# Half of a modulation in the output projection, transposes two tiles late, and six heads' softmax sums divided out of the gates

## The chip, the cores and the metric

The kernel runs on 1 core of one Trainium2 chip. The metric is the device time of one execution in microseconds (us); lower is better. A core has five engines with a queue of instructions each: TensorE (PE in the profile; its weight loads are PEld), VectorE (DVE), ScalarE (ACT), GpSimd (POOL), and SyncE (SP), which here issues the DMAs.

## The reference, cut to what matters

Two layers of a diffusion backbone, width 1024. There are 512 latent tokens and 256 context tokens (the context is updated in layer 0 only). Of each layer:

```
hx = rmsnorm(x) * (1 + scale_x) + shift_x        # shift, scale, gate = silu(c) @ w_ada + b_ada
px = hx @ w_in                                   # a_k a_v b_k b_v a_q b_q a_z b_z g_a g_b
qa, ka = rmsnorm per head; qb, kb = rope(rmsnorm per head)
a_att = neighbourhood attention of 8 heads, plus all context keys   # softmax(q k / 8 + bias) v
b_att = grouped attention of 8 query heads on 2 key heads           # softmax(q k / 8) v
o_a = (a_att * silu(a_z)) @ w_o_a;  o_b = (b_att * silu(b_z)) @ w_o_b
out = (sigmoid(g_a) * o_a + sigmoid(g_b) * o_b) @ w_out
x = x + gate_x * out
```

The context takes the same path in layer 0 with its own vector c_ctx and context keys alone. The shift and scale of layer 1 are needed when layer 1's hx is made, which is at the end of layer 0; its gate only at the end of layer 1.

## The kernel before, in words

**Products.** Every product with a weight is done in three passes (L346 to L348): both operands are split into a rounded high part and a low part. A weight tile of 128x512 arrives by DMA as `raw` (three buffers), ACT writes `whi` (L316, L331), and DVE or POOL writes `wlo` (L319, L333; `mix_lo` gives odd tiles to DVE, even ones to POOL). `tok_proj` (L356) makes 128 tokens by 512 columns in 24 matmuls; `chan_proj` (L362) makes channels by tokens. Results lie in PSUM tiles `psf` and `psx`, six in all outside the attentions.

**Stages of a layer.** (1) Products for a_k, a_v and a_q. A tile of a_k or a_q goes through `head_rstd` (ACT squares L386, DVE sums L388, POOL L253 and L255), a multiplication on DVE (L392), four transposes on PE and a copy on ACT (`to_channels`, L396 to L417). (2) Neighbourhood attention, below. (3) Products for b_k, b_v and b_q; these tiles get their rotation on DVE and POOL (`rope_heads`, L443 to L456) before the transposes. (4) Grouped attention. (5) The merge: products with w_o_b, then the output projection with w_out: two halves n of 512 columns with nt = 6 tiles of tokens each in layer 0; a finished tile is multiplied by the gate and added to x on DVE (L984, L986), and in the second half each tile's next-layer hx is made (`make_hx`, L258 to L279: ACT sum of squares, POOL, DVE y at L265, eight transposes L271 on PE, ACT with shift and scale, DVE split).

**An attention.** `pipeline` (L794) goes through 8 heads: scores of head h, then the values of head h-1, then some of `fill`, the independent products (gates a_z, b_z, g_a, g_b and, later, w_o_a), which are there to keep PE at work. For each of four query tiles, and two context tiles in layer 0, DVE takes the maximum (L755, L901, L687), ACT the exponentials with their sum `r` (L758, L903, L691), and `softmax_tail` (L607) scales p by 0.5/r: reciprocal on DVE (L609), then either one DVE operation (L612) or, for query tiles 1 and 3, two POOL operations (L614, L615). Then p is transposed on PE (L623, L625), split by ACT and DVE (`pth` L628, `ptl` L629), and multiplied with v (L778 to L789, L918, L919, L702, L703). `head_out` (L632) adds two halves and multiplies the gate z by the result on POOL (L639). The tiles p come from a pool of 7 buffers (neighbourhood attention, layer 0), 8 (layer 1) or 10 (grouped attention).

**The modulation.** Layer 1's shift and scale are 16 tiles of 128 outputs, and the 1024 inputs are taken in two halves. Of each half `ada_steps` (L200) makes 32 `dot` steps: a 256 KB tile `rawb` of w_ada is loaded (two buffers), and DVE multiplies and sums it with the row of c and the row of c_ctx, one step each (L222; the step with c_ctx overwrites rawb). The first half runs beside the products a_v and a_q of layer 0, the second half beside its neighbourhood attention (L831), followed by `ada_mod` (L237). The gate's 8 tiles run beside the grouped attentions.

**What sets the order.** A scheduler orders each engine's instructions when the program is built, by its own estimates of their durations; engines then run their queues strictly in that order. So an instruction whose input is late holds up everything behind it on its engine, SP's queue of DMAs included. Dots are pinned behind the last DVE instruction written before them.

Of the kernel before, what the change touches and what calls it, by code (L numbers as in the profile page):

```python
# [28 lines left out]
NA_POOL = (1, 3)  # L29
GQ_POOL = (1, 3)  # L30
# [17 lines left out]
def hybrid_kernel(es: ExitStack, tc, x, ctx, cvec, w_ada, w_ada0, small, gvec, w_in, w_o_a, w_o_b, w_out,  # L48
# [48 lines left out]

    x0, ctx0 = x[0], ctx[0]
# [4 lines left out]
    cd = drp.tile([16, 128], F32, name="cd")  # L103
    gs = [drp.tile([128, 4, NTOK], F32, name=f"gs{c}") for c in range(4)]
# [95 lines left out]
    def ada_steps(l, tiles, halves, nv, pool):  # L200
# [13 lines left out]
        def dot(h, i, v):  # L214
            if v == 0:
                load_tile(h, i)
            w = cb["w"]
            o = w if v == nv - 1 else pool.tile([128, 512], BF16, tag="junk", name=nm("junk"), bufs=1)
            ins = nc.cur_bb.bb.instructions
            before = next(j for j in reversed(ins) if j.engine == mybir.EngineType.DVE)  # L220
            n = len(ins)
            V.tensor_tensor_reduce(o, w, cb[h][:, v, :], 1.0, 0.0, ALU.mult, ALU.add, asum[:, i, h, v:v + 1])  # L222
            for j in nc.cur_bb.bb.instructions[n:]:
                if j.engine == mybir.EngineType.DVE:
                    tc.add_manual_dep(j, before.name, mybir.DependencyInfo(
                        mybir.DependencyClass.NoSync, mybir.DependencyReason.DATA), reason="program order")
# [151 lines left out]
    hp = {}  # L378
# [17 lines left out]
    def to_channels(y, npair, dst, t, perm, g):  # L396
# [46 lines left out]
    def rope_heads(npair, ps, rs, ta, tb, dst, t):  # L443
# [4 lines left out]
        r = hp["p"].tile([128, 512], F32, tag="rr", name=nm("rr"), bufs=2)  # L448
# [11 lines left out]
    def layer(l, hx, nxt, mid):  # L460
# [100 lines left out]
        if first:  # L561
# [13 lines left out]
            for t in range(6):  # L575
                ev(t, pss[t])
            bg = ada_steps(1, range(16), (0,), 2, hp["p"])
# [22 lines left out]
        for t in range(qt):  # L600
            tok_proj(w, 512, a_hx, t, evac_na(qav, True, gq, 5 if first else 2))
            run(bg, per_bg)
        run(bg, len(bg))
        bgp_es.close()

        if True:
            def softmax_tail(p, n, r, pieces, eng=None):  # L607

                V.reciprocal(r, r)  # L609
                for i, (c0, c1) in enumerate(pieces):  # L610
                    if eng is None:
                        V.tensor_scalar(p[:, c0:c1], p[:, c0:c1], r[:, i:i + 1], 0.5, ALU.mult, ALU.mult)  # L612
                    else:
                        G.tensor_scalar(r[:, i:i + 1], r[:, i:i + 1], 0.5, None, ALU.mult)  # L614
                        G.tensor_tensor(p[:, c0:c1], p[:, c0:c1],  # L615
                                        r[:, i:i + 1].to_broadcast([128, c1 - c0]), ALU.mult)
# [63 lines left out]
            def ctx_scores(q, kh, kl):  # L680
# [8 lines left out]
                r = sp.tile([128, 2], F32, tag="r", name=nm("r"), bufs=8)  # L689
                for i in range(2):  # L690
                    S.activation(p[:, 256 * i:256 * i + 256], pss[:, 256 * i:256 * i + 256], AF.Exp,  # L691
                                 bias=mx[:, i:i + 1], accum_out=r[:, i:i + 1])
                softmax_tail(p, 512, r, [(0, 256), (256, 512)])
# [25 lines left out]
            run(fill, PRE_NA * len(spans))  # L719
# [15 lines left out]
            def na_scores(h, q, kh, kl):  # L735
                load_bias(h)
                ps_ = []
                for i in range(4):
# [4 lines left out]
                    else:  # L743
# [7 lines left out]
                        for kk, b in ((kh, True), (kl, False)):  # L751
# [5 lines left out]
                    r = sp.tile([128, 2], F32, tag="r", name=nm("r"), bufs=8)  # L757
                    S.activation(p[:, :512], p[:, :512], AF.Exp, bias=mx[:, 0:1], scale=-1.0,  # L758
                                 accum_out=r[:, 0:1])
                    softmax_tail(p, 512, r[:, 0:1], [(0, 512)], G if i in NA_POOL else None)  # L760
# [33 lines left out]
            def pipeline(fill, spread, scores_of, values_of, last=None, bg=[]):  # L794
# [305 lines left out]
```

## Time and profile before

| | |
|---|---|
| Time, 3 runs | 1178.5 us median (1177.02 to 1178.72) |
| The profiled execution's own time | 1175.41 us |
| Span of the profiled execution | 1173.6 us |
| Granted TensorE clock, mean | 0.998 |
| PE matmuls | 6078 |
| DVE busy / POOL busy | 810.4 us / 507.5 us |
| ACT busy | 574.6 us |

The span runs from the first to the last instruction. Busy is the time in which an engine has an instruction in work. The matmuls' ends are modelled and matmuls overlap, so a PE that is shown busy may still have been held up for a little. "Idle before" is the time that an engine stood still ahead of an instruction, with what ended it. L-numbers are lines of the kernel before.

### The profile page before, as it was taken

What the parts mean: (1) busy time and instruction counts of PE and PEld (TensorE: products, weight loads), DVE (VectorE), ACT (ScalarE), POOL (GpSimd) and SP (SyncE); (2) the same over time, 40 slices, a digit from 0 to 9 for tenths busy, and PEclk for the clock granted to TensorE, in tenths of its full rate; (3) what the DMA queues carried; (4) which work ended last, traced back from release to release, by engine and by line L of the source; (5) the groups of instructions that cost most, each with busy time, mean ns of one, the idle gap of its engine ahead of it and who ended that gap; (6) DMA issues with size and microseconds to landing.
All of it is one profiled execution on the core that took longest, in us unless ns stands there. A gap on an engine that the chain in (4) does not pass through costs nothing.

```text
span 1173.6 us, 17342 instructions
## 1 busy us (share of the span) xinstructions
PE 1128.1 (96%) x6078; PEld 948.4 (81%) x6078; DVE 810.4 (69%) x1512; ACT 574.6 (49%) x1175; POOL 507.5 (43%) x463
## 2 busy tenths in 40 slices
PE   5999989899999999999999999999999999999898
PEld 4688878788997888878788887887888878877686
DVE  4557699986474599888583465339777657798573
ACT  4453254566452455576430264436656445756531
POOL 3362355453277244364410136336554764655311
PEclk9999999999999999999999999999999999999999
DMA  9534323321251443370240322413322525452133
GB/s 372 194 111 135 105 81 106 113 75 61 82 157 62 131 135 110 71 282 19 71 165 25 135 72 80 127 34 98 105 77 68 170 71 190 143 181 90 37 129 96
DMA packets 88128, 134.05 MB, mean 114 GB/s; under 512 B 10756, under 2 KB 52712, under 8 KB 86376
## 3 DMA queue, kind: packets, MB, share of 16 engines
q1 hardware_dynamic: 88040, 132.94, 35.4%
q8 instruction: 48, 0.79, 0.3%
q14 instruction: 40, 0.33, 0.1%
HBM read 115.58 MB, written 17.32 MB: 113 GB/s over the span
## 4 chain that ended last, share of the span: by engine, by line
PE 71%; DVE 14%; POOL 5%; issue 4%; ACT 3%; DMA 1%; DVEq 0%; POOLq 0%; ACTq 0%
PE psx L346 10%; PE psx L347 10%; PE psx L348 10%; PE psf L346 8%; PE psf L347 8%; PE psf L348 8%; PE pst L625 4%; DVE ptl L629 2%; PE pss L674 2%; PE pss L675 2%; PE psv L919 1%; POOL rsb L255 1%; DVE rawb L222 1%; DVE mx L901 1%; DVE qs L668 1%
## 5 line engine op out<-in xcount | busy, mean ns | idle before, releaser
L333 POOL TENSOR_TENSOR wlo<-raw,whi 128x512 fp32r<-128x512 f32 x64 | 91.5, 1432 | 121.9 <-ACT whi L331 101.8
L629 DVE TENSOR_TENSOR ptl<-pst,pth 128x512 fp32r<-128x512 f32 (+1 forms) x176 | 115.8, 671 | 40.8 <-ACT pth L628 39.8
L346 PE MATMUL psf<-hx,whi 128*128 128x512 f32 (+1 forms) x368 | 138.9, 378 | 1.1 <-DVE za L483 1.0
L347 PE MATMUL psf<-hx,whi 128*128 128x512 f32 (+1 forms) x368 | 138.3, 376 | 0.0
L348 PE MATMUL psf<-hx,wlo 128*128 128x512 f32 (+1 forms) x368 | 137.9, 375 | 0.0
L628 ACT CAST pth<-pst 128x512 fp32r<-128x512 f32 (+1 forms) x176 | 98.7, 577 | 79.4 <-PE pst L625 55.7
L346 PE MATMUL psx<-whi,hx 128*128 128x512 f32 (+1 forms) x368 | 136.4, 372 | 0.0
L347 PE MATMUL psx<-wlo,hx 128*128 128x512 f32 (+1 forms) x368 | 136.1, 370 | 0.0
L348 PE MATMUL psx<-whi,hx 128*128 128x512 f32 (+1 forms) x368 | 133.7, 370 | 0.0
L319 POOL TENSOR_TENSOR wlo<-raw,whi 128x512 fp32r<-128x512 f32 (+1 forms) x52 | 66.6, 1281 | 153.7 <-ACT whi L316 131.5
L316 ACT CAST whi<-raw 128x512 fp32r<-128x512 f32 (+1 forms) x112 | 64.7, 592 | 103.5 <-PE psx L348 36.5
L331 ACT CAST whi<-raw 128x512 fp32r<-128x512 f32 x128 | 78.0, 620 | 54.4 <-DMA raw<-in_w_in_dram 38.0
L625 PE MATMUL pst<-ident,p 128*128 128x128 f32 x640 | 100.3, 273 | 3.4 <-DVE ptl L629 1.1
L625 PEld LDWEIGHTS pst<-ident,p 128*128 128x128 f32 x640 | 77.8, 140 | 16.5 <-DVE p L612 1.3
L333 DVE TENSOR_TENSOR wlo<-raw,whi 128x512 fp32r<-128x512 f32 x64 | 63.9, 999 | 35.6 <-ACT whi L331 35.1
L615 POOL TENSOR_TENSOR p<-p,r 128x512 f32<-128x512 f32 (+1 forms) x64 | 86.3, 1348 | 5.2
L614 POOL TENSOR_SCALAR r<-r 128x1 f32<-128x1 f32 x64 | 24.5, 383 | 135.2 <-DVE r L609 127.3
L346 PEld LDWEIGHTS psf<-hx,whi 128*128 128x128 f32 x368 | 69.5, 189 | 12.9 <-DVE za L483 1.7
L319 DVE TENSOR_TENSOR wlo<-raw,whi 128x512 fp32r<-128x512 f32 (+1 forms) x60 | 49.5, 828 | 43.1 <-ACT whi L316 42.3
L346 PEld LDWEIGHTS psx<-whi,hx 128*128 128x128 f32 x368 | 69.4, 189 | 11.8 <-issue 0.8
L348 PEld LDWEIGHTS psf<-hx,wlo 128*128 128x128 f32 x368 | 69.4, 189 | 11.6
L348 PEld LDWEIGHTS psx<-whi,hx 128*128 128x128 f32 x368 | 69.6, 189 | 11.2
(239 smaller groups left out, 3068.1 us busy)
## 6 DMA issues: line engine op xcount, KB each, us to landing
raw<-in_w_in_dram SPq DMA_DIRECT2D x160, 256.0 KB, 2.9
rawb<-in_w_ada_dram SPq DMA_DIRECT2D x64, 256.0 KB, 2.7
gs<-zt SPq DMA_DIRECT2D x32, 256.0 KB, 2.4
raw<-in_w_out_dram SPq DMA_DIRECT2D x32, 256.0 KB, 2.6
tg<-gs SPq DMA_DIRECT2D x4, 1536.0 KB, 7.1
rawx<-in_w_ada_dram SPq DMA_DIRECT2D x4, 1024.0 KB, 6.5
rawy<-in_w_ada_dram SPq DMA_DIRECT2D x4, 1024.0 KB, 12.2
raw<-in_w_o_a_dram SPq DMA_DIRECT2D x16, 256.0 KB, 3.1
```

The source lines that it names most:

```text
L316: S.copy(hi[:, :n], raw[:, :n])
L319: e.tensor_tensor(lo[:, :n], raw[:, :n], F(hi[:, :n]), ALU.subtract)
L331: S.copy(hi, raw)
L333: lo_eng(i).tensor_tensor(lo, raw, F(hi), ALU.subtract)
L346: T.matmul(ps, lhs[0], rhs[0], start=first, stop=False)
L347: T.matmul(ps, lhs[0], rhs[1], start=False, stop=False)
L348: T.matmul(ps, lhs[1], rhs[0], start=False, stop=last)
L614: G.tensor_scalar(r[:, i:i + 1], r[:, i:i + 1], 0.5, None, ALU.mult)
L615: G.tensor_tensor(p[:, c0:c1], p[:, c0:c1], r[:, i:i + 1].to_broadcast([128, c1 - c0]), ALU.mult)
L625: T.transpose(pt[:, c0:c0 + 128], src, ident)
L628: S.copy(hi[:, n0:n1], pt[:, n0:n1])
L629: V.tensor_tensor(lo[:, n0:n1], pt[:, n0:n1], F(hi[:, n0:n1]), ALU.subtract)
```

## The change

Three things are changed, and a few buffer counts with them.

1. The second half of layer 1's modulation (one load of the rows c, 32 dots, `ada_mod`) leaves layer 0's neighbourhood attention and goes into layer 0's output projection: 6 steps after each of the first tiles of half n = 0, so that all are written there. Dots are now pinned by the new helper `behind`, which does for any engine what the old lines did for DVE.
2. The transposes of a_k, a_q, b_k and b_q are written later: `to_channels` puts them in a list, and `tok_proj` writes out the oldest when more than two wait, so that a tile's transposes stand two products behind its own product (in layer 0 from a_q on; a_k's six there stay where they were). They are pinned on PE behind the last PE instruction written before them. At the end of a stage the remaining two follow the first fill pieces.
3. For heads 0 to 5 of each attention the exponentials stay unscaled. The sums of a pair of heads are collected in one tile r; `invert` makes 0.5/r on DVE, `sums_out` turns it by one PE transpose, copies it on ACT and writes it to DRAM by a DMA on ACT's queue; a head later `normalise` reads it back with SP DMAs that repeat each head's row on 64 partitions, into a buffer of the pool of p, and POOL multiplies the pair's gated output z by it. Heads 6 and 7 scale every tile of p on DVE; POOL scales none.

```diff
+    def behind(fn):
...
+    def turn_late(n):
+        while len(hp["late"]) > n:
+            after_products(hp["late"].pop(0))
-    def to_channels(y, npair, dst, t, perm, g):
+    def to_channels(*a):
+        hp["late"].append(lambda: turn(*a))
+    def turn(y, npair, dst, t, perm, g):
...
         tok_mm(ps, w, n, a, t, 0, KT)
         evac(t, ps)
+        turn_late(hp["lag"])
...
-                tok_proj(w, 512, a_hx, t, evac_na(kav, False, gk))
+                tok_proj(w, 512, a_hx, t, evac_na(kav, False, gk, 4))
...
+        for i in range(PRE_NA * len(spans)):
+            run(fill, 1)
+            turn_late(1 if i == 0 else 0)
+        turn_late(0)
...
-            def softmax_tail(p, n, r, pieces, eng=None):
-                V.reciprocal(r, r)
...
+            def scale(h, p, r, c0, c1):
+                if h > 5:
+                    V.reciprocal(r, r)
+                    V.tensor_scalar(p[:, c0:c1], p[:, c0:c1], r, 0.5, ALU.mult, ALU.mult)
+            def invert(r):
+                n = 6 if first else 4
+                V.tensor_scalar(r[:, 0:n], r[:, 0:n], 2.0, None, ALU.mult)
+                V.reciprocal(r[:, 0:n], r[:, 0:n])
+            def sums_out(j, r):
+                n = 12 if first else 8
+                pt = psw(128, "t")
+                T.transpose(pt[0:n], r[:, 0:n // 2].rearrange("p j e -> p (j e)"), ident)
+                row = p_tile()[:, 0:128]
+                S.copy(row[0:n], pt[0:n])
+                S.dma_start(rd[j][0:n], row[0:n])
+            def normalise(j, z, perm):
...
+                    rb = p_tile()[:, 0:128 * (j1 - j0)]
+                    for e in range(2):
+                        nc.sync.dma_start(rb[64 * e:64 * e + 64].rearrange("p (j q) -> p j q", q=128),
+                                          rd[j].rearrange("(j e) q -> e j q", e=2)[e:e + 1, j0:j1]
+                                          .to_broadcast([64, j1 - j0, 128]))
...
+                        G.tensor_tensor(zp, zp, rb, ALU.mult)
...
                     if prev is not None:
                         values_of(h - 1, prev)
+                    if h % 2 and h < 7:
+                        invert(att["r"])
+                        sums_out(h // 2, att["r"])
+                    elif h % 2 == 0 and h:
+                        behind(lambda: normalise(h // 2 - 1, z, perm))
...
-            bg = ada_steps(1, range(16), (1,), 2, att["p"]) + [lambda: ada_mod(1)] if first else []
-            run(bg, 1)
-            pipeline(fill, 9, na_first, values_of(za, na_values), bg=bg)
+            pipeline(fill, 9, na_first, values_of(za, na_values), za, True)
...
-            run(fill, PRE_GQ * len(spans))
+            for i in range(PRE_GQ * len(spans)):
+                run(fill, 1)
+                turn_late(1 if i == 0 else 0)
...
+            bg = ada_steps(1, range(16), (1,), 2, mp) + [lambda: ada_mod(1)] if first else []
+            run(bg, 1)
+            per_bg = -(-len(bg) // nt)
             for n in range(2):
...
                     tok_proj(w, 512, a_m, t, evac_o)
+                    run(bg, per_bg)
                     run(late, len(late) - 1)
```

More of the change, by code (lines that the diff above doesn't have):

```diff
@@ L103, in hybrid_kernel @@
     cd = drp.tile([16, 128], F32, name="cd")
+    rd = [drp.tile([12, 128], F32, name=f"rd{i}") for i in range(4)]
     gs = [drp.tile([128, 4, NTOK], F32, name=f"gs{c}") for c in range(4)]
@@ L218, in dot @@
             o = w if v == nv - 1 else pool.tile([128, 512], BF16, tag="junk", name=nm("junk"), bufs=1)
[L219 to L226, printed above, removed]
+            behind(lambda: V.tensor_tensor_reduce(o, w, cb[h][:, v, :], 1.0, 0.0, ALU.mult, ALU.add,
+                                                  asum[:, i, h, v:v + 1]))
         res = []
@@ L576, in layer @@
                 ev(t, pss[t])
+            for fn in hp["late"]:
+                fn()
+            hp["late"] = []
+            hp["lag"] = 2
             bg = ada_steps(1, range(16), (0,), 2, hp["p"])
@@ L939, in layer @@
             run(bg, 1)
-            pipeline(fill, 8, gq_first, values_of(zb, gq_values), early, bg)
+            pipeline(fill, 8, gq_first, values_of(zb, gq_values), zb, False, early, bg)
             gq_es.close()
```

89 lines of the change are left out of this document (59 added, 30 removed).

## The prediction

> **What bounds the kernel now.** I read the page's busy line and its chain first.
>
> ```profile
> span 1173.6 us, 17342 instructions
> PE 1128.1 (96%) x6078; PEld 948.4 (81%) x6078; DVE 810.4 (69%) x1512; ACT 574.6 (49%) x1175; POOL 507.5 (43%) x463
> ...
> PE   5999989899999999999999999999999999999898
> ...
> PE 71%; DVE 14%; POOL 5%; issue 4%; ACT 3%; DMA 1%; DVEq 0%; POOLq 0%; ACTq 0%
> ```
>
> PE is the bound: busy 96%, and the chain of waits that ended last runs on it for 71%. No part of the change takes matmuls away, so it can win only where PE stands still: 1173.6 - 1128.1 = 45.5 us. The view by stretches says where (the stretch and its length, then busy time and, in brackets, instructions of PE, PEld, DVE, ACT and POOL, the granted clock, DMA's share and GB/s).
>
> ```profile
> 150.00:235.00 85.00, 76.52 (x456) 65.90 (x455) 83.12 (x183) 44.44 (x101) 39.84 (x31) 1.00 0.35 104
> 235.00:325.00 90.00, 90.00 (x587) 81.25 (x586) 58.41 (x131) 51.49 (x120) 36.02 (x38) 1.00 0.24 77
> 425.00:525.00 100.00, 96.58 (x588) 84.04 (x587) 88.68 (x162) 59.38 (x125) 44.62 (x37) 1.00 0.49 150
> ```
>
> Some of it lies in the start, which the change doesn't touch (the first slice of the strip is a 5). The largest gap behind it that I found is the first half of layer 0's neighbourhood attention: 8.5 us of PE idle in 150 to 235 us, with DVE busy 83.1 of 85; in its second half, without dots, DVE falls to 58 of 90 and PE never stops. What PE waited for, in layer 0's neighbourhood attention, its grouped attention with the end of b_q, and layer 1's two attentions:
>
> ```profile
> PE pst L623 <- DVE ptl L629: 4.7, 2, 3.2
> PE pss L674 <- DVE za L483: 1.3, 1, 1.3
> PE pst L625 <- POOL p L615: 1.0, 1, 1.0
> PE pst L625 <- DVE p L612: 0.7, 1, 0.7
> PE pss L752 <- DVE mx L755: 0.5, 1, 0.5
> ```
>
> ```profile
> PE psv L919 <- DVE ptl L629: 1.1, 3, 0.6
> ...
> PE pst L401 <- DVE rr L451: 0.9, 1, 0.9
> ...
> PE pst L625 <- DVE r L609: 0.6, 1, 0.6
> PE pst L401 <- DVE rr L456: 0.2, 1, 0.2
> ```
>
> ```profile
> PE pst L401 <- DVE rr L456: 2.6, 2, 1.3
> PE psv L918 <- ACT pth L628: 1.2, 1, 1.2
> PE pst L625 <- DVE ptl L629: 1.1, 3, 0.6
> PE pst L623 <- DVE ptl L629: 1.1, 2, 0.8
> ```
>
> A stop costs a little more than its idle time:
>
> ```profile
> 222.18 0.28 PE L348 MATMUL psx<-hx,wlo 128*128 128x256 f32 x1
> 222.30 0.28 PE L346 MATMUL psx<-hx,whi 128*128 128x256 f32 x1
> 225.80 0.33 PE L623 MATMUL pst<-ident,p 128*128 128x128 f32 x1 [3.22 <-DVE ptl L629]
> ```
>
> These matmuls start 0.12 us apart though each is shown 0.28 long, so 0.16 us of every stop hides under a modelled end: here 3.50 - 0.12 = 3.38 us were lost, not 3.22. Stops under 0.16 us don't show at all.
>
> **Part 1a: the dots leave the neighbourhood attention; part 3 there.** DVE's work from 150 to 325 us, three stretches with L222, L612 and L609 alone, and then the groups of the last two by shape (busy time, mean ns of one, idle before):
>
> ```profile
> 150.00:325.00 175.00, 29.33 (x64) 1.00 0.29 90
> 150.00:325.00 175.00, 18.51 (x32) 1.00 0.29 90
> 150.00:325.00 175.00, 6.12 (x40) 1.00 0.29 90
> ```
>
> ```profile
> L612 DVE TENSOR_SCALAR p<-p,r 128x512 f32<-128x512 f32 x16 | 11.3, 707 | 0.3
> L612 DVE TENSOR_SCALAR p<-p,r 128x256 f32<-128x256 f32 x16 | 7.2, 489 | 0.1
> L609 DVE RECIPROCAL r<-r 128x1 f32<-128x1 f32 x32 | 4.8, 154 | 2.8 <-ACT p L758 2.6
> ```
>
> Gone: 29.3 + 18.5 + 6.1 = 53.9 us. Back come heads 6 and 7: 8 x 0.707 + 4 x 0.489 + 12 x 0.154 = 9.5 us, and 6 small operations of `invert`, about 1 us. DVE goes from 83.1 + 58.4 = 141.5 us to about 98 of 175, and POOL loses its two operations per scaled tile. The stops on ptl, p (twice) and mx go: 6.9 us of idle in 5 stops, 7.7 with 0.16 each; I take **-9** with smaller ones and some that don't show. The stop on za (1.3) is the entry, where the last transposes of a_q, the copy and the staging of q follow each other: it stays. Bounds: -5 (half of the stops pass to ACT's pth) to -10.
>
> **Part 3 in layer 0's grouped attention.** Its own 32 dots stay and keep DVE at 88.7 of 100 in 425 to 525 us. Three stops on ptl and one on r go, 1.7 + 4 x 0.16 = 2.3; with unseen ones **-3**, between 0 and -6.
>
> **Part 2.** The changed order puts 23 or 24 matmuls between one tile's transposes and the next in a_q, and 18 to 32 in b_q; a tile is given two products. The four stops on rr, 3.7 us, are gone, with 0.16 each **-4.3** (-2 to -5). What is late next: the scores behind the last transposes, which wait for copy and staging. In layer 1's grouped attention 22 matmuls cover that where 19 did, in layer 0's neighbourhood attention 24 + 14 where 13 + 24 did; nothing is added. The first four tiles of layer 1's a_k keep their place, so their stops stay.
>
> **Part 3 in layer 1.** Of the stops in the third list I give back 1.5 us. The end of the grouped attention (1070 to 1105 us) has no fill left, and there heads 6 and 7 put 4 more scalings on DVE, where POOL did them: +1 for these. Net **-0.5**, between -6 and +2.
>
> **What part 3 adds.** PE gets 12 transposes of the sums. Eight transposes start at 665.28 and the next matmul at 666.07:
>
> ```profile
> 665.28 1.04 PE L271 MATMUL pst<-ident,y 128*128 128x128 f32 x8
> 666.07 0.48 PE L346 MATMUL psx<-whi,mh 128*128 128x512 f32 x1
> ```
>
> 0.1 us each, **+1.2** in all. Each waits for `invert`, and that for ACT's last sum; behind it on PE are the fill and the next transposes, and in the changed order other work stands between. 12 copies and DMA issues on ACT (busy 49%) and 12 groups of multiplications on POOL in place of 128 operations are hidden. The sums' way through DRAM isn't in the trace; the nearest rows are two small writes (cd, gd) and a read (bint), each with its size and the median time from issue to landing:
>
> ```profile
> bint<-in_bias_int_dram SPq DMA_DIRECT2D x16, 128.0 KB, 2.1
> ...
> cd<-csl SPq DMA_DIRECT2D x1, 8.0 KB, 5.9
> gd<-ag SPq DMA_DIRECT2D x1, 8.0 KB, 11.3
> ```
>
> Write and read take 5.9 + 2.1 = 8 to 11.3 + 2.1 = 13.4 us, beside a head of (325 - 150)/8 = 22 us between write and read: 0. Without that cover POOL would wait for the read with `kl` (L658) and `wlo` (L333) behind it, and PE for these. The Trainium skill (DMA: Bandwidth & Descriptors, Anatomy of one DMA, measured there for DMAs that GpSimd issues) speaks against such a trip: about 2 us fixed for each DMA, mostly the receipt of the write, heaviest for HBM. Two crossings would be 4 us, an estimate by that page, and the sum the same; the small writes here took longer than it says.
>
> **Part 1b: the dots in the output projection.** DVE there, before:
>
> ```profile
> 621.20:656.70 35.50, 35.50 (x159) 29.39 (x158) 12.53 (x17) 4.97 (x8) 5.51 (x4) 1.00 0.19 60
> ```
>
> ```profile
> 660.25 0.75 DVE L265 TENSOR_SCALAR y<-xt,rsb 128x1024 f32<-128x1024 f32 x1 [0.87 <-POOL rsb L255]
> ```
>
> From the first finished tile (621.2) until the first tile of half 2 (656.7) DVE is free 35.5 - 12.5 = 23.0 us; its y ends at 661.0 and PE wants it at 665.3: 4.3 more, 27.3 in all. A dot:
>
> ```profile
> L222 DVE DVE_READ_ACCUMULATOR2_ANT asum<- x112: 71/80/86, 92.5 to 1040.3; 128x1 f32 x112
> L222 DVE CUSTOM_DVE_ANT_0 rawb<-rawb,cb x64: 662/692/2183, 92.6 to 1039.3; 128x512 f32<-128x512 f32 x64
> ```
>
> 32 x (0.69 + 0.08) + 0.5 for `ada_mod` = 25.1 us at the median, which fits; at the sum in the attention, 29.3 + 0.5, PE would wait 2.5 us. POOL works only 5.5 of these 35.5 us, so I take the median. By the Trainium skill (SBUF — State Buffer, SBUF: two separate sides) DVE operations with two SBUF inputs and POOL lock each other out for a whole instruction; the spread from 0.66 to 2.18 us agrees, and by it the dots would be short here. The second limit is the load of rawb: 2 buffers, 16 loads.
>
> ```profile
> rawb<-in_w_ada_dram SPq DMA_DIRECT2D x64, 256.0 KB, 2.7
> ```
>
> ```profile
> SPq L212 <- DVE asum L222: 98.8, 46, 11.7
> ```
>
> Each load is issued when the dots have freed a buffer. A buffer's round is 2.7 + 1.5 us of dots + about 0.4 to issue = 4.6, so 2.3 us per load at two buffers: 16 take about 37 us, in which the evacuations partly fit. From 621.2 to the y transposes less y's own 4.3 us there are 39.8. I take **+1**, from 0 to +4. Behind a waiting dot on DVE stand the evacuations and the odd `wlo` of half 2, behind a waiting load on SP the weights of half 2; PE waits for both.
>
> **Sum.** -9 - 3 - 4.3 - 0.5 + 1.2 + 1 = -14.6 us. The profiled execution took 1175.4 us, so 1160.8; the median of the runs, 1178.5, is 3.1 above it, so **1164**. The bounds of the terms give -26.8 to +0.2.
>
> **Rivals.**
> - **The loads pace the output projection: slower.** If each of the 16 loads is paid in full, 4.6 us, they take 73 us, 33 over the 39.8: 1164 + 33 - 1 = 1196. From 2.5 us per load PE waits, from 39.8/16 + 15.6/16 = 3.5 us the gain is eaten. For it: two buffers, and SP's queue in order with weights between the loads; the attention's SP waited up to 11.7 us for a dot. Against it: three loads per tile of 35.5/6 = 5.9 us ask for 2.0 us each, and DMA is at 0.19 there. 0.12.
> - **The stops pass on.** DVE is relieved, but PE then waits for ACT's pth and the exponentials, which are as many as before; only part 2's stops stay away, with a little of part 1a: -4 to -7, 1173. For it: pth and p L903 are already in the lists. Against it: ACT is busy 44 of 85 us where DVE is at 83. 0.2.
> - **Nearly all idle in the attentions goes**, hidden stops with it: -25, 1153. For it: 235 to 325 us shows a stretch without a stop when DVE has air. 0.15.
> - **The change doesn't lift the load**: p's buffers, of which the sums and their copies take 3 per pair of heads, beside 10 tiles of p in 7 buffers, or POOL's wait for the read, give 1 us back in each of 12 rounds: 1176 to 1178. 0.06. (By the page's 4 us it would be less.)
>
> The forecast, 1157 to 1170, keeps 0.47. The range 1151 to 1177 takes it, the second and third rival but for their ends, and some of the last. A measurement can tell 0.2% (2.4 us): faster 0.79, within 0.07, slower 0.14.
>
> **What would show it.** Right: PE idle in the first 85 us of the first attention under 3 us with DVE under 60; no wait of L401 on rr; the eight y transposes without idle before them; a span near 1159. Wrong: PE idle before the first y transposes or at half 2's matmuls, with DVE waiting for rawb; or PE waits on pth in place of ptl.

## The result, and the profile after

The changed kernel takes **1183.7 us** (median of 13 runs, 1180.8 to 1189.6), the kernel before 1177.7 (13 runs beside them): ratio 1.0051, 95% interval 1.0041 to 1.0062, so 6.0 us slower. The forecast was 1164 with a range of 1151 to 1177. The profiled execution took 1181.4 us.

The page of the changed kernel: the busy line, and the strips of PE and of its granted clock.

```profile
span 1179.6 us, 17147 instructions
PE 1130.4 (96%) x6090; PEld 952.0 (81%) x6090; DVE 758.0 (64%) x1376; ACT 577.0 (49%) x1187; POOL 405.1 (34%) x356
PE   5999999999999999999799999999998999999898
PEclk9999999999999999999899999999999999999999
```

DVE has lost 52 us and POOL 102, as the change means them to, and PE is idle for 1179.6 - 1130.4 = 49.2 us where it was 45.5. In the 20th slice PE has a 7 and its clock an 8; the kernel before has 9 in both. The stretches that the prediction named, and those where the time went (columns as in the prediction: the stretch and its length; PE, PEld, DVE, ACT, POOL; the clock):

```profile
150.00:235.00 85.00, 85.00 (x536) 76.14 (x534) 61.74 (x108) 56.67 (x128) 32.16 (x23) 1.00 0.24 75
235.00:325.00 90.00, 88.98 (x585) 80.49 (x584) 50.07 (x110) 46.06 (x111) 29.23 (x32) 1.00 0.29 89
425.00:525.00 100.00, 99.46 (x612) 87.70 (x611) 75.32 (x123) 63.30 (x134) 32.69 (x23) 1.00 0.44 145
550.00:575.00 25.00, 18.76 (x101) 15.85 (x100) 15.86 (x16) 6.79 (x12) 8.55 (x6) 0.80 0.24 83
600.00:660.00 60.00, 60.00 (x282) 50.11 (x281) 50.04 (x111) 11.08 (x20) 8.80 (x6) 1.00 0.43 141
875.00:925.00 50.00, 44.97 (x303) 39.74 (x302) 36.26 (x89) 28.37 (x72) 20.23 (x27) 1.00 0.30 91
1050.00:1105.00 55.00, 47.89 (x250) 36.29 (x248) 43.08 (x70) 35.12 (x68) 13.20 (x10) 1.00 0.23 75
```

The last rows of the kernel before:

```profile
550.00:575.00 25.00, 25.00 (x161) 22.11 (x160) 17.51 (x32) 15.12 (x31) 8.70 (x8) 1.00 0.07 22
600.00:660.00 60.00, 60.00 (x287) 50.53 (x286) 32.24 (x53) 13.25 (x24) 8.88 (x8) 1.00 0.27 93
875.00:925.00 50.00, 48.58 (x322) 43.05 (x321) 36.58 (x82) 27.70 (x68) 24.82 (x31) 1.00 0.30 90
1050.00:1105.00 55.00, 51.17 (x272) 39.40 (x271) 43.46 (x71) 34.39 (x66) 23.45 (x22) 1.00 0.19 63
```

So idle went where it was expected: 8.5 us in the first half of the first attention, 2.9 in the grouped attention, and PE is not idle in this stretch of the output projection although DVE's work there rose from 32.2 to 50.0 us. New idle stands in three places: 6.2 us, with a low clock, at the end of layer 0's grouped attention (550 to 575 us), 5.0 where it was 1.4 from 875 to 925 us (the end of layer 1's first attention), and 7.1 where it was 3.8 from 1050 to 1105 us (the end of its second).

Idle in a fixed window isn't yet time lost, because the two kernels don't do the same work in it. So take four marks that every kernel has, the first score matmul (into `pss`) of each attention, and the time from one to the next in the profiled executions, in us:

| | layer 0, first attention to grouped | layer 0, grouped, to layer 1's first | layer 1, first to grouped | layer 1, grouped, to the end |
|---|---|---|---|---|
| before | 245.3 | 396.4 | 171.6 | 208.1 |
| changed | 235.5 | 402.7 | 172.0 | 215.9 |

The first stretch gained 9.8 us. The second lost 6.3 and the fourth 7.8. Layer 1's first attention lost only 0.4, in spite of its idle.

**The first place.** POOL, DVE and PE of the changed kernel there, one view each:

```profile
559.94 0.73 POOL L709 TENSOR_TENSOR zb<-zb,ho 64x256 f32<-64x256 f32 x1 [3.03 <-DVE ho L708]
560.63 5.35 POOL L552 TENSOR_TENSOR gbl<-zb,gbh 128x768 fp32r<-128x768 f32 x3
565.94 1.26 POOL L341 TENSOR_TENSOR wlo<-raw,whi 128x512 fp32r<-128x512 f32 x1
```

```profile
560.89 6.87 DVE L341 TENSOR_TENSOR wlo<-raw,whi 128x512 fp32r<-128x512 f32 x1
567.67 1.27 DVE L699 TENSOR_TENSOR ptl<-pst,pth 128x512 fp32r<-128x512 f32 x2
```

```profile
561.75 0.41 PE L996 MATMUL psv<-pth,vb 128*128 128x512 f32 x1
568.40 0.80 PE L997 MATMUL psv<-ptl,vb 128*128 128x512 f32 x1 [6.24 <-DVE ptl L699]
569.00 0.63 PE L996 MATMUL psv<-pth,vb 128*128 128x512 f32 x1
569.42 1.06 PE L695 MATMUL pst<-ident,p 128*128 128x128 f32 x4
```

A subtraction that takes DVE 0.69 us as a rule (the median of its 64 in this profile) ran for 6.87 us, until 0.55 us after the last of four POOL operations that followed each other without a gap; `ptl` stood behind it in DVE's queue, and PE behind `ptl`. Read the last fence on: before the stop a 512-column matmul is shown 0.41 us long, behind it 0.63 to 0.80. The one at 569.00 is followed after 0.42 us, where 0.23 is usual. The clock by stretches:

```profile
562.00:564.00 2.00, 0.16 (x1) 0.00 (x0) 2.00 (x1) 0.10 (x1) 2.00 (x2) 1.00 0.00 0
564.00:565.00 1.00, 0.00 (x0) 0.00 (x0) 1.00 (x1) 0.00 (x0) 1.00 (x2) 0.58 0.00 0
565.00:568.00 3.00, 0.00 (x0) 0.00 (x0) 3.00 (x2) 0.00 (x0) 2.20 (x2) 0.50 0.00 0
568.00:574.00 6.00, 5.60 (x17) 4.61 (x18) 1.94 (x4) 1.17 (x2) 0.00 (x0) 0.50 0.69 237
574.00:575.00 1.00, 1.00 (x6) 0.78 (x6) 0.39 (x1) 0.00 (x0) 0.00 (x0) 0.80 0.26 102
575.00:576.00 1.00, 1.00 (x7) 0.72 (x5) 0.03 (x1) 0.59 (x1) 0.00 (x0) 1.00 0.12 49
```

The clock is halved while PE waits and stays halved for about 6 us after PE goes on; 5.6 us of work at half speed cost another 2.8. The 13 runs of the changed kernel have mean clocks of 0.988 to 0.995, slower runs mostly the lower ones; those of the kernel before 0.993 to 0.999. The kernel before has the same three `gbl` operations one behind the other, and there DVE, asking 0.6 us after their start, got in after the first and was done in 1.78 us:

```profile
569.20 0.73 POOL L639 TENSOR_TENSOR zb<-zb,ho 64x256 f32<-64x256 f32 x1 [1.27 <-DVE ho L638]
573.53 5.88 POOL L523 TENSOR_TENSOR gbl<-zb,gbh 128x768 fp32r<-128x768 f32 x3 [3.60 <-PE psf L347]
```

```profile
574.14 1.78 DVE L333 TENSOR_TENSOR wlo<-raw,whi 128x512 fp32r<-128x512 f32 x1
```

### The profile page after: what moved, and what is told of

Its sections match the earlier page's. It is cut to its first block, busy times and chain, and to the rows that moved or that the text cites. A ratio compares the mean times of both kernels' runs of the same rounds, so it can differ in the third digit from the quotient of the medians.

```text
span 1179.6 us, 17147 instructions
## 1 busy us (share of the span) xinstructions
PE 1130.4 (96%) x6090; PEld 952.0 (81%) x6090; DVE 758.0 (64%) x1376; ACT 577.0 (49%) x1187; POOL 405.1 (34%) x356
## 5 line engine op out<-in xcount | busy, mean ns | idle before, releaser
L341 POOL TENSOR_TENSOR wlo<-raw,whi 128x512 fp32r<-128x512 f32 x64 | 89.0, 1395 | 188.0 <-ACT whi L339 170.1
L341 DVE TENSOR_TENSOR wlo<-raw,whi 128x512 fp32r<-128x512 f32 x64 | 69.1, 1080 | 51.1 <-ACT whi L339 47.9
L354 PEld LDWEIGHTS psf<-hx,whi 128*128 128x128 f32 x368 | 69.5, 189 | 14.2 <-ACT zt L510 3.9
L354 PEld LDWEIGHTS psx<-whi,hx 128*128 128x128 f32 x368 | 69.5, 189 | 11.7 <-issue 0.8
L355 PEld LDWEIGHTS psx<-wlo,hx 128*128 128x128 f32 x368 | 69.8, 190 | 10.8
L355 PEld LDWEIGHTS psf<-hx,whi 128*128 128x128 f32 x368 | 69.5, 189 | 10.0
```

What stands on the lines that cost most here:

```text
L341: lo_eng(i).tensor_tensor(lo, raw, F(hi), ALU.subtract)
L354: T.matmul(ps, lhs[0], rhs[0], start=first, stop=False)
L355: T.matmul(ps, lhs[0], rhs[1], start=False, stop=False)
```

## The experiments

All times are medians; the ratio is to the kernel before on the same chip, where that had 1177.1 to 1178.2 us. "us" is the ratio times 1177.8, less 1177.8.

| kernel | median | ratio (95%) | us |
|---|---|---|---|
| changed (parts 1, 2, 3) | 1183.7 | 1.0051 (1.0041 to 1.0062) | +6.0 |
| e1 low parts of gated b on DVE | 1181.9 | 1.0034 (1.0019 to 1.0048) | +4.0 |
| e2 heads 6, 7 scaled with POOL | 1185.8 | 1.0066 (1.0047 to 1.0084) | +7.8 |
| e3 dots back in the attention | 1189.2 | 1.0097 (1.0073 to 1.0121) | +11.4 |
| e4 layer 1 without part 3 | 1172.4 | 0.9947 (0.9929 to 0.9965) | -6.2 |
| e5 e4, w_o_b's low parts on POOL | 1165.4 | 0.9889 (0.9870 to 0.9908) | -13.1 |
| e6 part 2 alone | 1173.6 | 0.9963 (0.9950 to 0.9977) | -4.4 |
| e7 layer 1: two pairs unscaled | 1183.3 | 1.0046 (1.0029 to 1.0062) | +5.4 |
| e9 parts 1 and 2, no part 3 | 1165.3 | 0.9885 (0.9867 to 0.9904) | -13.5 |
| e10 own buffers for sums, layer 1 | 1178.6 | 1.0006 (0.9992 to 1.0019) | +0.7 |
| e12 e9, w_o_b's low parts on POOL | 1167.4 | 0.9906 (0.9890 to 0.9922) | -11.1 |
| e14 e10, w_o_b's low parts on POOL | 1171.0 | 0.9948 (0.9931 to 0.9964) | -6.1 |
| e15 context product on DVE | 1179.1 | 1.0013 (1.0002 to 1.0024) | +1.5 |
| e16 e4, context product on DVE | 1165.6 | 0.9901 (0.9883 to 0.9918) | -11.7 |

Two theories stood at first. **Collision:** the stop at 561 us with its low clock is the loss. **Layer 1:** what part 3 does at the ends of layer 1's attentions is the loss. The prediction's own slower rival (loads of rawb pace the output projection) was the third.

**e1.** POOL's train is taken away: its three low parts go to DVE.

```diff
-            hilo(zb, gated["b"], range(3))
+            hilo(zb, gated["b"], range(3), V)
```

> The changed kernel, but the low parts of the gated output b (three operations of 128x768, L552, that POOL did one behind the other) are made on DVE. Collision theory: in the profile of the changed kernel one DVE subtraction (wlo L341, 560.9 us) ran 6.87 us beside four POOL operations that followed each other without a gap, PE stood still for 6.4 us behind it and then ran at half clock until 574.8 us; together 9.8 us of that stretch were lost where the kernel before lost 0.7. Without the POOL train the stall and the low clock go, DVE gets about 3 us more: 7 to 10 us faster than the changed kernel, 1174 to 1177 where the changed kernel has 1184, and no stretch of clock under 0.9 between 550 and 600 us. Theory of layer 1 (the scaling of heads 6 and 7 on DVE costs most there): 1183 to 1185, for nothing is changed there but the same operations, which get 2 us slower.

1181.9, 2 us better at most. The 6.87 us operation and the low clock at 565 us are gone, but DVE, three operations longer, made PE wait 2.1 us there, and in the profiled execution the clock fell to 0.70 and 0.62 in the two slices of 5 us from 890 us, and to 0.77 from 975 to 980, instead. By the marks the stretch with the collision is 5.2 us shorter (397.5 us), and layer 1's two stretches are 1.8 and 2.8 longer. The edit moves the three low parts in layer 1 too, so e1 isn't a test of the collision alone; e15 and e16 come nearer to one.

**e2.**

```diff
+                    if i in (1, 3):
+                        G.tensor_scalar(r, r, 0.5, None, ALU.mult)
+                        G.tensor_tensor(p[:, c0:c1], p[:, c0:c1], r.to_broadcast([128, c1 - c0]), ALU.mult)
+                        return
```

> The changed kernel, but of heads 6 and 7 the query tiles 1 and 3 are scaled on POOL again. Theory of layer 1: PE's stalls from 875 to 925 us and from 1025 to 1125 us, 8.7 us more than before, come from DVE, which scales all tiles of these heads; with POOL's help 4 to 8 us come back: 1176 to 1180 where the changed kernel has 1184. Collision theory: these stalls are the ends of attentions without fill, where DVE, ACT and POOL are each late by turns; -2 to +1, and the 9.8 us at 561 us stay as long as the four POOL operations follow each other there.

1185.8: no gain. The scalings of heads 6 and 7 on DVE, for which the prediction had allowed +1, are not what layer 1 lost.

**e3.** The diff is the change's lines for the dots, reversed: they stand in the first attention again.

> The changed kernel, but the second half of the modulation goes back into layer 0's neighbourhood attention; scaling and transposes stay as changed. If the dots in the output projection pace it (the slower rival of the prediction), the output projection of layer 0 gets faster by more than 3 us and the whole too: 1179 or less. If they cost 1 us there, as the traces say (1.3 us of PE stalls between 600 and 700 us against 0.3), the attention gets some of its stalls back, 2 to 8 of the 10.6 us, and the whole is 1 to 7 us slower: 1185 to 1191.

1189.2, 5.5 us slower: the second branch. By the marks the first attention's stretch is 4.9 us longer (240.4 us where it was 235.5). The slower rival of the prediction is out.

**e4.**

```diff
-                if h > 5:
+                if h > 5 or not first:
...
-                    if h % 2 and h < 7:
+                    if not first:
+                        pass
+                    elif h % 2 and h < 7:
```

(and POOL scales query tiles 1 and 3 in layer 1, as in e2)

> The changed kernel, but layer 1 scales its exponentials as before (every tile, POOL for query tiles 1 and 3, no sums through DRAM). Theory of layer 1: the 8.7 us of stalls that layer 1's attentions have got go: 1175 to 1178 where the changed kernel has 1184. Collision theory: layer 1 gives back 0 to 4 us: 1180 to 1184, and the 9.8 us in layer 0 stay.

1172.4: 11 to 12 us better, more than the theory of layer 1 asked, and the collision in layer 0 is untouched (PE idles 6.2 us from 550 to 575 us, and the clock is 0.86). Both theories hold, each for its part.

**e5, e6, e7, e8.** The edit of e5:

```diff
-                    st["w"] = load_w2(src, 256 * i, 4, mix_lo)
+                    st["w"] = load_w2(src, 256 * i, 4, pool_lo if first and br == "b" else mix_lo)
```

> Layer 1 scales its exponentials as before, and in layer 0 POOL makes all low parts of the weights w_o_b, so that DVE has no subtraction of two SBUF tiles beside the POOL train at 561 us. Collision theory: against the same kernel with the DVE subtraction (1172.4) the 6.4 us stall and the half clock behind it go, POOL's own longer queue costs 0 to 3: 1163 to 1167, PE stalls between 550 and 600 us under 6 us instead of 12, clock 1.00 there. If the stall only moves on (POOL late with these weights): 1170 to 1175, with PE waiting for wlo from POOL.

1165.4, 7 us below e4, the clock 1.00: as the collision theory says. e6 is the kernel before with the diff's lines of `late`, `turn` and `turn_late`, and the buffer counts that go with them:

> The kernel before with the late transposes alone (part 2). By the prediction's term: -4.3 us (-2 to -5), 1173 to 1176 where the kernel before has 1178, and no stop of the transposes on rr. Theory after the traces: the changed kernel's transposes still stop for 5.4 us on rr (before 4.8), in more and smaller pieces, for rotation on DVE and POOL is what is late, not the transposes early; part 2 is worth -1 to +2: 1177 to 1180, and the stops of the transposes sum to 4 us or more.

1173.6: the time that the prediction gives part 2 was right, and my theory from the traces wrong. The prediction's reason for it was not: layer 1's stops on rr, about 3 us, are still there. e7:

```diff
-                if h > 5:
+                if h > 5 or (h > 3 and not first):
```

> The changed kernel, but in layer 1 only the first two pairs of heads stay unscaled; heads 4 to 7 scale every tile on DVE, and the last way of sums through DRAM is 2 heads farther from the end. Theory of the end (the third pair's sums, their buffers and POOL's multiplications stand in the way of the last two heads): most of the 8.4 us of layer 1 come back, 1175 to 1178 where the changed kernel has 1184. Theory of the whole part (any pair costs its share, or the new order does): 1180 to 1185.

1183.3, as the whole part: it isn't the third pair's nearness to the end. e8 measures the collision by itself.

> No layers are computed (the output is a copy of x): 1, 2, 4 or 6 POOL subtractions of 128x768 without a gap, and beside them on DVE a short operation of 32 to 512 columns that sets the moment of arrival, and then a subtraction of 128x512 with two SBUF inputs, or a scaling with one, or a subtraction with one input in PSUM. If DVE always gets in at the next seam between two POOL operations: at most 1.8 + 0.65 = 2.5 us for the subtraction, whatever the train's length. If POOL keeps what they share as long as its next operation is ready: the subtraction takes the rest of the train, 6 to 7 us beside 4 and 9 to 11 us beside 6. If it hangs on the moment of arrival, both are seen, sorted by the columns. With one SBUF input or PSUM: under 1 us beside any train.

DVE's subtraction of two SBUF tiles ended 2.39 to 2.40 us after its case began in all 40 cases, beside trains of several lengths, and whether DVE's own instruction started 0.06 or 0.56 us after the train: always 0.55 us after the first POOL operation's end. A scaling with one SBUF input waited as well (20 of 20), a subtraction with one input in PSUM never (0.68 us, 20 of 20). One of them beside a train of six:

```profile
160.05 11.52 POOL L51 TENSOR_TENSOR t<-a,b 128x768 fp32r<-128x768 f32 x6 [0.35 <-ACT a L49]
160.11 2.29 DVE L54 TENSOR_TENSOR t<-a,b 128x512 fp32r<-128x512 f32 x1
```

(This bench's POOL operations have 0.08 us between them; in e11 they follow each other without one, with the same result.) So the rule is that DVE gets in at the next seam, and the 6.87 us is an exception that needed a cause. The Trainium skill (SBUF — State Buffer, SBUF: two separate sides) says that such a DVE operation and a GpSimd operation lock each other out for one whole instruction; this bench agrees for a train of full operations, and the case at 561 us doesn't: four instructions.

**e9, e10, e11, e12.** e9 scales everything as before and keeps parts 1 and 2:

> The changed kernel without part 3 in both layers: every exponential is scaled as before, with POOL for query tiles 1 and 3; dots in the output projection and late transposes stay. The prediction's term for the first attention was -9 for dots and scaling together. If the dots alone were the load there: 5 to 9 us below the kernel with the late transposes alone (1173.6), so 1165 to 1169, with PE stalls between 150 and 235 us under 4 us (before 12.6, changed 2.0). If the scaling carries most of it: 1170 to 1174, and stalls of 6 us or more there. Either way without a collision at the end of layer 0's grouped attention if that one came with part 3's order.

1165.3: the first branch, the fastest kernel of the study together with e5 and e16. Its first attention, dots gone and scaling kept:

```profile
150.00:235.00 85.00, 85.00 (x535) 76.25 (x534) 72.20 (x152) 55.54 (x125) 44.63 (x41) 1.00 0.23 69
425.00:525.00 100.00, 97.21 (x591) 84.78 (x590) 87.54 (x160) 59.67 (x127) 46.15 (x40) 1.00 0.46 136
```

DVE at 72 of 85 us is enough for PE never to idle. e10:

```diff
-                row = p_tile()[:, 0:128]
+                row = p_tile()[:, 0:128] if first else att["p"].tile([128, 128], F32, tag="row", bufs=1)
...
-                    rb = p_tile()[:, 0:128 * (j1 - j0)]
+                    rb = p_tile() if first else att["p"].tile([128, 512], F32, tag="rb", bufs=1)
```

> The changed kernel, but in layer 1 the sums' copy and the read-back rows have buffers of their own and no longer take turns with the tiles of exponentials (8 in the neighbourhood attention). If these buffers hold up layer 1's last heads there: PE stalls from 875 to 925 us fall from 8.6 to about 5 (before 4.7), 1179 to 1181 where the changed kernel has 1184. If it is only the new order: 1182 to 1185.

1178.6, 5 us better. Against the changed kernel's row for 875 to 925 us, e10:

```profile
875.00:925.00 50.00, 48.19 (x316) 41.96 (x315) 35.21 (x84) 27.05 (x67) 21.21 (x27) 1.00 0.30 91
```

Idle is 1.8 us here, where the changed kernel had 5.0 and the kernel before 1.4. So a row and its read-back do take buffers that the tiles p need: my reading is that the next head's tiles then wait until the head before has been transposed, which no view here shows. The edit gives both of layer 1's attentions their own buffers, and the marks in the profiled executions put 0.5 us of its gain in the first and 1.9 in the grouped one; how the 5 us divide isn't settled. e11 looks for the exception:

> No layers are computed (the output is a copy of x): four POOL subtractions of 128x768 behind one another, alone, or behind a short one on 64 partitions, or with the third reading what the first wrote, as around the 6.87 us in the changed kernel; DVE's subtraction of two SBUF inputs asks at moments 0.1 to 5.5 us after the train's start. If one of these makes POOL keep the others out to the end of the train, some cases end 4 to 7 us after asking; if not, each ends by the next seam, 0.65 to 2.5 us after asking, and what happened at 561 us stays without a cause.

72 of 72 got in at the next seam with a train alone or with the third operation reading the first's result (DVE asked 0.06 to 0.56 us after the train's or the leader's start in all cases; e13 has later moments). With a 64x256 operation in front, **36 of 36 were kept out until the train's end**, 7.58 us after that operation. e12:

> As the kernel without part 3, and POOL makes all low parts of w_o_b in layer 0. If there is a collision like that at 561 us in it, it goes and 6 to 9 us with it; if there is none, within 1.5 us of the kernel without part 3.

1167.4: no gain, so there was no collision in e9 to take away. It is 2 us slower by the medians, and the intervals overlap.

**e13, e14.** e13 varies the train's leader.

> No layers are computed (the output is a copy of x): the train of four POOL subtractions of 128x768, led by one operation of another form: 64 partitions (lower or upper half; 256, 512 or 768 columns; multiplication or subtraction), 32 partitions, or 128 partitions with 64, 256 or 512 columns; DVE's operation asks during the leader or in the first two operations behind it. If it is the leader's 64 partitions that keep DVE out to the train's end (asked and kept out 36 of 36 times behind 64x256), all forms on 64 partitions do it and none on 128; if it is that it is short, 128x64 and 128x256 do it and 64x768 doesn't; if it needs DVE's asking in the leader, the later moments get in at the next seam, which would leave the case in the changed kernel (asked in the operation behind the leader) open.

| leader | DVE kept out to the train's end |
|---|---|
| 64x256 on partitions 0 to 63, product or difference | 20 of 20 (4 of them scalings with one input) |
| 64x512 on partitions 0 to 63 | 8 of 8 |
| 32x512 on partitions 0 to 31 | 8 of 8 |
| 64x768 on partitions 0 to 63 | 0 of 8 |
| 64x256 on partitions 64 to 127 | 0 of 8 |
| 128x64, 128x256, 128x512 | 0 of 24 |

Two of its cases, leader in the lower half and in the upper half; DVE asks at the same moment, 1.13 us after the leader's start:

```profile
34.64 0.72 POOL L50 TENSOR_TENSOR h<-h,a 64x256 f32<-64x256 f32 x1 [0.98 <-ACT a L54]
...
35.33 7.07 POOL L57 TENSOR_TENSOR w<-a,b 128x768 fp32r<-128x768 f32 x4
35.77 7.17 DVE L62 TENSOR_TENSOR t<-a,t 128x512 fp32r<-128x512 f32 x1
```

```profile
174.15 0.72 POOL L50 TENSOR_TENSOR h<-h,a 64x256 f32<-64x256 f32 x1 [0.35 <-ACT a L54]
...
174.96 7.53 POOL L57 TENSOR_TENSOR w<-a,b 128x768 fp32r<-128x768 f32 x4
175.28 2.02 DVE L62 TENSOR_TENSOR t<-a,t 128x512 fp32r<-128x512 f32 x1
```

None of the three readings fits whole: not every 64 partitions, not shortness, and not the moment of asking (0.18 to 2.58 us after the leader's start, in the cases kept out and in those that got in). What all 36 have is a leader that leaves the upper partitions out and is narrower than 768 columns, with no gap behind it.

Two of these stay mixed. In the upper half's cases the train started 0.08 us after the leader's end, in those kept out 0.03 to 0.04 us before it, so half and gap aren't separated; the 64x768 and the 128-partition leaders have no gap either, so for them the gap isn't it. And such a leader isn't enough: in layer 0's first attention a product of 64x512 (head 6 again) is followed without a gap by a 128x256 low part on POOL, and DVE's 128x256 subtraction, asked for during the product, got in at the first seam in the changed kernel and eleven others (in the changed one the product starts at 288.93 us, the low part at 290.17, and the subtraction runs from 289.38 to 290.49). That the leader has to be narrower than what follows it would fit all of these, and wasn't tried.

In the changed kernel the leader is the gate product of the context part of head 6 (`head_out`, L709), an even head, so partitions 0 to 63, 256 columns (the trace doesn't show partitions; on PE the last head's values follow it). In the kernel before, POOL had stood idle for 3.6 us between that product and the train, because the train's first operation waited for PE's last fill product (`psf`, in the fence of the kernel before); e6 and e9 have the same 3.6 us. In the changed kernel that product's last matmul starts at 560.03 us, before the gate product has ended, and nothing stands between. So part 3 in layer 0 (e4 against e9) closed the gap; which piece of its new order did it isn't separated.

> The changed kernel with all three parts, own buffers for the sums in layer 1, and POOL making all low parts of w_o_b in layer 0. Own buffers gave 5 us (1178.6), the collision 7: 1170 to 1173 if the two add up. If part 3 were worth its 3.5 us of stalls in layer 0 and layer 1's cost were its buffers alone: 1162 to 1165, as fast as without part 3 (1165.3) or faster.

1171.0: the two add up, and layer 1 keeps a loss of its own.

**e15, e16** put the eight context products of layer 0's grouped attention, the leader among them, on DVE.

```diff
-                G.tensor_tensor(dst, dst, t1[m:m + 64, :n], ALU.mult)
+                (V if att["w"] == 768 and n == 256 else G).tensor_tensor(dst, dst, t1[m:m + 64, :n], ALU.mult)
```

> The changed kernel, but in layer 0's grouped attention the product of the gate with the context part of a head (64x256, the form that led the POOL train at 561 us) is made on DVE; the train of three low parts and one weight's low part stays on POOL. By the bench, a train led by a 128-partition operation lets DVE in at the next seam: no DVE operation of over 3 us, PE stalls between 550 and 600 us fall from 12.5 to under 7, clock 1.00 there, 1174 to 1179 where the changed kernel has 1184. If the leader doesn't matter in the kernel: the 6.87 us stays, 1183 to 1186.

1179.1, and the same subtraction beside the same train, POOL's view and DVE's:

```profile
561.18 5.94 POOL L552 TENSOR_TENSOR gbl<-zb,gbh 128x768 fp32r<-128x768 f32 x3 [2.89 <-PE psf L355]
```

```profile
560.94 0.42 DVE L709 TENSOR_TENSOR zb<-zb,ho 64x256 f32<-64x256 f32 x1
561.28 0.41 DVE L586 SCALAR_TENSOR_TENSOR tg<-tg,psf 128x256 f32<-128x256 f32 x1
561.79 1.83 DVE L341 TENSOR_TENSOR wlo<-raw,whi 128x512 fp32r<-128x512 f32 x1
```

The three `gbl` start at 561.18 us, DVE asks 0.6 us later and is in at the first seam: 1.83 us. Without the leader on POOL the exception is gone in the kernel too.

> The same product on DVE, with layer 1 scaling its exponentials as before. By the bench: the kernel with layer 1's old scaling (1172.4) less the collision, 1163 to 1166, at or a little under the kernel without part 3 (1165.3), for part 3 keeps 3.5 us fewer stalls in layer 0's grouped attention and pays 1 to 2 for transposes and copies. If the leader doesn't matter: 1172 to 1174.

1165.6, 5.5 us below e4. It isn't faster than e9: part 3 in layer 0, freed of the collision, is worth nothing that can be measured (e16 is 1.8 us above e9, e5 2.0 below e12, and both pairs' intervals overlap).

**What is left in layer 1.** Part 3 costs 12.2 us there (changed less e4). Own buffers give 5.3 back. The last two columns of the marks say where it lies:

| | layer 1, first to grouped | layer 1, grouped, to the end |
|---|---|---|
| without part 3 in layer 1: before, e4, e5, e6, e9, e12, e16 | 171.0 to 171.6 | 207.6 to 208.1 |
| with it, own buffers: e10, e14 | 171.1 to 171.5 | 213.7 to 214.0 |
| with it: changed, e1, e2, e3, e7, e15 | 171.0 to 176.4 | 215.9 to 225.2 |

So the loss lies mainly in the grouped attention, and own buffers leave about 6 us of it there. (The 172.8 and more of e1, e2, e3 and e15 come with a low clock from about 890 us on.) The wait of PE at the entry of layer 1's grouped attention, e10 (e4 has only the first):

```profile
PE pst L430 <- DVE rr L485: 2.8, 4, 1.3
PE psf L354 <- ACT zt L510: 2.7, 1, 2.7
```

This second stop, 2.5 to 2.9 us, is in all eight kernels of the study with part 3 in layer 1 and in none of the other six, nor before. In the changed kernel it reads: SP issues two loads of rawb at 969.0 us, when a dot has freed their buffer, and only then the weights, at 970.9 us (in e4 a weight's load stands between the two, at 969.5 us); ACT's cast of a weight waits 2.1 us for them and the evacuation `zt` stands behind it. In e10 the clock was 0.66 from 975 to 980 us, behind that stop. What remains lies in small stops up to 1105 us, whose cause I haven't separated from the new order.

## Why the prediction was wrong, step by step

- **Part 1a, -9, and part 1b, +1: right.** e9 less e6 is -9.1 us against -8 forecast. Idle in the first 85 us of the attention went from 8.5 to 0, DVE from 83.1 to 61.7. The marks divide the two terms: from e6 to e9 the first attention's stretch falls by 9.2 us (243.5 to 234.3) and the stretch with the output projection grows by 0.8 (395.9 to 396.7). Only the explanation was too wide: the dots alone do it. The scaling's departure adds nothing once the dots are gone (235.5 in the changed kernel); with the dots kept it would have brought 3.1 us (240.4 in e3). DVE's work from 150 to 325 us came to 111.8 us, not the 98 forecast; PE's idle there was 0 and 1.0 us all the same.
- **Part 2, -4.3: right in size, not in place.** e6 measures -4.4. Of the stops on rr, those in layer 0 shrank from 1.1 to 0.2 us in e6; layer 1's stayed at 2.8 where they had been 2.6. The marks don't place the rest: in e6's profile the first attention's stretch is 1.8 us shorter, the way to it 0.9 longer and the last three stretches 0.5, 0.4 and 0.2 shorter, which is 2.0 of the 4.4 in these single executions. Since the stops that were to go stayed for the most part, the agreement in size is in good part luck. In the changed kernel itself the stops on rr sum to 3.9 us (1.6 in layer 0, 2.3 in layer 1) against 3.7: "no wait of L401 on rr" was wrong.
- **Part 3 in layer 0's grouped attention, -3: the stops went, 2.9 us, and came back at its end.** The step that failed is "where a stall goes, say what is late next": I had POOL relieved and did not ask what its later operations would stand next to. The last gate product now ended after PE's last fill product, so the wait of 3.6 us between it and the three low parts was gone and they closed up to a train; that train and its leader cost 4.5 to 7 us of time (e15, e16, e5), and the term measured +7.3 (e4 less e9) where -3 was forecast.
- **Part 3 in layer 1, -0.5: the step that failed most.** It measures +12.2, outside its own range of -6 to +2. I priced four scalings, which cost nothing to speak of (e2), and left buffers to a rival at 0.06 that gave 1 us back in each of 12 rounds. The buffers cost 5.3 us in layer 1 alone (e10), and the weights of a fill piece that come late 2.5 to 2.9. The rest of the 12.2, some 4 us if these two add up, lies in the grouped attention too (e10 and e14 keep about 6 us there), and its cause is open.
- **What part 3 adds, +1.2:** not separated. The reads of the sums took medians of 2.6 us (64 KB), 2.9 (128 KB) and 10.3 (192 KB) where 2.1 was taken; no wait of PE or POOL names them, so the trip was hidden as forecast.
- **The sum:** the lower bounds add up to -25.8, not -26.8; the range would have begun at about 1152, and nothing hangs on it.
- **The rivals.** The slower one had the wrong mechanism: the loads of rawb paced nothing, and DVE's waits for them in the output projection, 5.3 us in 7 cases, cost PE no idle time, but for 0.5 us before the first y transposes ("without idle before them" was wrong by that). The right answer, 1184, lay above the range because both terms of part 3 came out beyond their bounds (+7.3 where 0 was the bound, +12.2 where +2 was), and because no term held the clock: a stop of 6 us cost PE another 2.8 at half speed.

The sum as measured: -9.1 (part 1) - 4.4 (part 2) + 12.2 (part 3 in layer 1) + 7.3 (part 3 in layer 0, e4 less e9) = +6.0. Each term is the difference of two of the runs, so that they add up says nothing more.

## What to carry to other kernels

Relieving an engine that isn't the bound pays only in the stretch where it ends the wait: here the dots' 29 us were enough, and the scalings that part 3 took off DVE and POOL bought nothing on top. Before the order on an engine's queue is changed, look at what its gaps wait for: where the new order has that wait over earlier, operations close up to a train, and another engine may need the gap. Bound each part against its own stage and each buffer against the stage with the fewest; and add to any stop of several us the slow clock behind it.

## What the runs showed of the hardware

- DVE operations that read SBUF with two inputs, or a 512-column scaling with one, wait for the POOL operation in progress and get in at the next seam (60 of 60 in e8, with 0.08 us between POOL's operations; 72 of 72 in e11 without); one input in PSUM doesn't wait. **But behind a POOL operation on the lower partitions only (32 or 64, 256 or 512 columns), they wait for the whole train that follows without a gap** (72 of 72 in e11 and e13, and 6.87 us to within 0.02 in six kernels of the study). A leader of 64x768 (0 of 8), one in the upper half (0 of 8, but with 0.08 us behind it) and one of 64x512 before a narrower 128x256 operation (twelve kernels) don't do it; why is open.
- The clock fell to half 2.0 us after PE's last matmul (it ended at 562.16 us, and a mean of 0.58 from 564 to 565 us puts the fall at about 564.2) and returned 6.0 us after PE went on (568.4 us, and a mean of 0.80 from 574 to 575 us puts the return at about 574.4): 10.2 us at half. Smaller stops can do it in some executions: 2.2 us with a further 0.8 close before, at 890 us, in e1's profile, and not in the changed kernel's with the same stops. The Trainium skill (TensorE: Matmul & The Clock Gate, What's actually happening) says that the gate goes by a window of about 3.4 us that runs free of the program; that fits the chance from run to run, and the 10.2 us are about three such windows.
